# Norm factors of the attention input applied behind the products, in a two-layer trunk on one core

## The chip, the cores and the metric

One Trainium2 chip, one of its cores. The metric is the device time of one execution in microseconds (us). Before the change: median 762.31 us of 3 runs (762.25 to 763.36). The engines are TensorE (PE; PEld is its weight load), VectorE (DVE), ScalarE (ACT), GpSimd (POOL) and SyncE (SP). Each works through its own list of instructions in the order in which they were written down, and waits where an instruction's input is not ready.

## The reference

Two layers on 256 tokens of width 1024. Each layer normalises its input, multiplies it by one wide matrix, runs two attentions and gates, then a SwiGLU block:

```python
def rms_norm(x, g):
    y = x * rsqrt(mean(x * x, axis=-1) + EPS)     # token factor r, one per token
    return y * g                                  # column factor, one per column

h = rms_norm(x, attn_norm)
aq, ak, av, iq, ik, iw, bq, bk, bv, gates = split_cols(h @ w_in)
aq = apply_rope(rms_norm(aq, a_q_norm), cos, sin)         # 8 heads of 64; ak, bq, bk alike
iq = apply_rope(iq, cos, sin)                             # indexer: 4 heads of 64
ik = apply_rope(rms_norm(ik, idx_k_norm), cos, sin)
ya = sparse_attention(aq, ak, av, iq, ik, iw * 0.5, k_sel)  # 64 keys of each query by indexer score
yb = diff_attention(bq, bk, bv, lam)                      # then a norm per head
g_a, g_b = split(sigmoid(gates + gate_bias))
x = x + (g_a * (ya @ w_up_a) + g_b * (yb @ w_up_b)) @ w_out
h = rms_norm(x, ffn_norm)
gate, up = split(h @ w_ffn_in)
x = x + (silu(gate) * up) @ w_ffn_out
```

## The kernel before, in words

The 256 tokens stand in two tiles of 128, t = 0 and 1. A product is made from transposed activations (128 columns of the model and 128 tokens at a time) and weight units of 512 columns. For accuracy each fp32 product is three: both operands are split into a rounded high part and the rest, and `mm3` adds high·high (L240), high·low (L241) and low·high (L242). Activations are split after the transpose (`hilo`, or `hi` and `lo` in the first block), weights after their load: `split_half` makes the high part on ACT (L149) and the low part on DVE (L150). Raw weights lie in four buffers `raw`, split ones in four pairs `wh`, `wl`.

Names in the rows: a letter pair and a layer and a token tile, so `aq00` is the a-queries of layer 0, tile 0. `a0T` and `a1T` are the banks of the transposes of the attention input of layers 0 and 1, `a0h` and `a1h` the normalised input before it, `a0Th` and `a0Tl` the split halves. `gA`, `gB` are the gates, `ix` the indexer block (324 columns), `av`, `bv` the values, `fo` the last matrix of the SwiGLU.

Front of layer 0. The gain row is loaded to one partition and spread over 128 by a product with ones (`g0`, L374). For each token tile ACT sums the squares (L378), POOL makes r (L273, L276: a sum and a power), and DVE multiplies x by r and the gain (`norm_scale`, L309). PE transposes the result (L249), 4 chunks of 128 to a bank; ACT takes the high part of a whole bank (L713), DVE the low part (L716). The first block is half of gate A (`gA`), then `ix`. This stretch is in an order written out by hand for ACT and DVE (`first_block`); `part` makes the products of some chunks for one token tile.

Behind it comes a list of blocks for each layer (`BLOCKS`: ak, aq, av, bk, gA1, bq, bv, gB0, uA, gB1, uB). PE's order is the order of the program: `tok_block` makes a tile's product, hands the bank to an evacuation (`evac`), and `later` and `tick` put follow-up work on PE a set number of steps later (`QK_T` = 4 steps for the transposes of q and k). The instructions of the other engines are put in order by a scheduler outside the kernel from its own estimates, so a change of one place can change the order of DVE and ACT at others. Each of q and k ends in `qk_finish`: 8 sums of squares on ACT (one per head, L466), a power on POOL, for k a product by the factor on DVE (L471), for q a scaling of the factor (L474), then the rotation `rope` in three DVE steps (L455, L456, L458), and the transpose on PE. The indexer's finish (`idx_finish`) is alike; its scores are cut to the top 64 by eight rounds of `MAX` and `MATCH_REPLACE` on DVE (L529, L530), for two token tiles, `sc00m` on `nb` of tile 0, `sc01m` on that of tile 1.

At the end of layer 0 each half of x gets its `fo` product added (L920), ACT sums squares, POOL makes r, and `norm_scale` runs before the transposes of layer 1 (`a1T`).

Of the kernel before, what the change touches and what calls it, by code (L numbers as in the profile page):

```python
# [18 lines left out]
P = 128  # L19
# [17 lines left out]
GATE = IDX + IDXW + 1536  # L37

# [48 lines left out]
def tile_trunk(ctx, tc, x, angle, wpk, widx, gnorm, gbias, gqk, dlam, subln, const, out):  # L87
# [165 lines left out]
    cst = cp.tile([P, 3 * P], F32, name="cst")  # L253
    ident, cb = cst[:, :P], cst[:, P:3 * P]
# [3 lines left out]
    def load_x(t):  # L258
        nc.sync.dma_start(xs[t], x[0, t * P:(t + 1) * P, :])
# [38 lines left out]

    def norm_sum(N, t):
# [4 lines left out]
    def norm_scale(N, t, *parts):  # L304
        r = N["r", t]
        for c in parts or range(2):
            cs = slice(512 * c, 512 * c + 512)
            N["h"][t, c] = t2k([P, 512], f"{N['name']}h{t}{c}")
            nc.vector.scalar_tensor_tensor(N["h"][t, c], xs[t][:, cs], r, N["g"][c], ALU.mult, ALU.mult)  # L309

# [56 lines left out]
    g0b = [bank(f"g0{c}") for c in range(2)]  # L367

    def heat(n):
        nc.tensor.matmul(warm[:, :n], lhsT=idle[:, :P], rhs=idle[:, :n], start=True, stop=True)  # L370
# [12 lines left out]
    nc.gpsimd.dma_start(cb, const[:, P:])  # L383
# [11 lines left out]
    def angles():  # L395
        ve = nc.gpsimd
        ve.tensor_copy(posf, posi)
# [86 lines left out]
    def idx_finish(acc, l, t, I):  # L484
# [3 lines left out]
        nc.vector.tensor_scalar(iw, acc[:, 320:324], 0.5, None, ALU.mult)  # L488
        r = small(1, name + "r")
        nc.scalar.activation(junk[:, :64], acc[:, 256:320], AF.Square, scale=0.125, accum_out=r)  # L490
# [4 lines left out]
        nc.vector.tensor_scalar(kn, acc[:, 256:320], r, None, ALU.mult)  # L495
# [11 lines left out]
    def indexer(l, t, I):  # L507
# [10 lines left out]
        for j in range(2):  # L518
# [3 lines left out]
            nc.scalar.activation(rv, dv, AF.Relu, scale=0.125)  # L522
# [172 lines left out]
    def first_block(name, xT, evacs):  # L695
# [11 lines left out]
        def trans(t, g):  # L707
            b = bank(f"a0T{t}{g}")
            transposes(b, NA["h"][t, g], range(4))
            return [a[:, 4 * g:4 * g + 4, t * P:(t + 1) * P] for a in NA["T"]], heads(b, 4)  # L710

        def hi(d, b):
            nc.scalar.activation(d[0], b, AF.Copy)  # L713

        def lo(d, b):
            nc.vector.tensor_tensor(d[1], b, d[0].bitcast(F32), ALU.subtract)  # L716

        d0 = trans(0, 0)
        d1 = trans(1, 0)
        split_half(parts=2, between=lambda: (hi(*d0), lo(*d0)))  # L720
        hi(*d1)
        lo(*d1)
        split_half(parts=2)
        part(0, 0)
        part(0, 1, 0, 2)
        norm_scale(NA, 0, 1)
        split_half()
        d0 = trans(0, 1)
        hi(*d0)
        lo(*d0)  # L730
        part(0, 1, 2, 2)
        norm_scale(NA, 1, 1)
        split_half()
        part(1, 0, 0, 2)
        d1 = trans(1, 1)
        hi(*d1)
        lo(*d1)
        for _ in range(3):
            split_half()
        sines(turns)  # L740
        split_half()
# [13 lines left out]
    for l in range(DEPTH):  # L755
# [28 lines left out]
        def v_fin(i, t):  # L784
            return lambda acc: nc.scalar.activation(V8[i][:, t, :], acc, AF.Copy)
# [24 lines left out]
        def g_fin(g, c, t):  # L810
# [6 lines left out]
            def f(acc):  # L817
                nc.vector.tensor_tensor(G[0][:, t, cols[c]], acc, gb[g, c], ALU.add)
# [196 lines left out]
        for t in range(NT):  # L1015
            for c in range(2):
# [81 lines left out]
```

## Time and profile before

| | |
|---|---|
| median of 3 runs | 762.31 us (762.25 to 763.36) |
| profiled execution | 762.28 us |
| its span, first to last instruction | 760.5 us |
| PE busy | 751.3 us (99%) |
| PE weight load | 617.0 us (81%) |
| DVE busy | 573.6 us (75%) |
| ACT busy | 470.6 us (62%) |
| POOL busy | 108.7 us (14%) |
| HBM read | 152.89 MB, 202 GB/s over the span |

Busy shares are over the span. A matmul's time in the trace is longer than the distance to the next, since matmuls overlap in a pipeline; the distance between starts is what a product costs PE. An entry in square brackets behind a row is the time that the engine stood idle before it and what released it.

### The profile page before, as it was taken

How to read it: one execution, taken by the hardware profiler on the slowest of the kernel's cores; microseconds unless marked ns; L12 is line 12 of the kernel's file. 1: busy time of each engine (PE TensorE's matmuls, PEld its weight loads, DVE VectorE, ACT ScalarE, POOL GpSimd, SP SyncE). 2: the span in 40 equal slices, each digit the busy share in tenths (PEclk: the TensorE clock that was granted, in tenths of full speed). 3: DMA queues.
4: the chain of work that ended last, by engine and by line, in shares of the span. 5: the costliest groups of instructions: out<-in, count | busy, mean ns of one | idle time of the engine just before them, and what ended most of it. 6: DMA issues, size and time to landing. Idle time of an engine off the chain costs nothing.

```text
span 760.5 us, 10268 instructions
## 1 busy us (share of the span) xinstructions
PE 751.3 (99%) x3638; PEld 617.0 (81%) x3638; DVE 573.6 (75%) x885; ACT 470.6 (62%) x938; POOL 108.7 (14%) x135
## 2 busy tenths in 40 slices
PE   8999999999999999999999999999999999999998
PEld 5877888888888888888888787888888888888886
DVE  5999757768777777777768987667777877787673
ACT  5766597655665656656547676876546666565660
POOL 5741220010031100010001411200002010000100
PEclk9999999999999999999999999999999999999999
DMA  9744635436568888977746273443476599868921
GB/s 317 290 168 166 235 125 183 162 115 234 206 167 264 234 275 258 275 231 221 240 150 221 91 242 125 177 170 125 166 272 213 152 218 293 255 236 270 231 102 55
DMA packets 45061, 154.60 MB, mean 203 GB/s; under 512 B 5409, under 2 KB 6177, under 8 KB 45010
## 3 DMA queue, kind: packets, MB, share of 16 engines
q1 hardware_dynamic: 40320, 136.97, 49.1%
q0 software_dynamic: 4688, 16.98, 12.7%
q8 instruction: 28, 0.46, 0.2%
q14 instruction: 23, 0.19, 0.1%
q10 hardware_dynamic: 2, 0.00, 0.0%
HBM read 152.89 MB, written 1.05 MB: 202 GB/s over the span
## 4 chain that ended last, share of the span: by engine, by line
PE 90%; DVE 5%; ACT 1%; DMA 1%; POOL 1%; issue 1%; SPq 0%; ACTq 0%; DVEq 0%
PE fo L242 5%; PE fo L240 5%; PE fo L241 5%; PE fi L242 5%; PE fi L241 5%; PE fi L240 5%; PE qX L242 3%; PE qX L240 3%; PE qX L241 3%; PE gB L240 2%; PE gB L242 2%; PE wo L242 2%; PE gB L241 2%; PE wo L240 2%; PE wo L241 2%; PE gA L240 2%
## 5 line engine op out<-in xcount | busy, mean ns | idle before, releaser
L240 PE MATMUL fo<-wh,aTh 128*128 128x512 f32 (+1 forms) x100 | 38.2, 382 | 0.0
L241 PE MATMUL fo<-wl,aTh 128*128 128x512 f32 (+1 forms) x100 | 38.1, 381 | 0.0
L242 PE MATMUL fo<-wh,aTl 128*128 128x512 f32 (+1 forms) x100 | 38.1, 381 | 0.0
L197 ACT ACTIVATE wh<-raw1q 128x1024 fp32r<-128x1024 f32 (+1 forms) x24 | 30.0, 1268 | 8.3 <-DMA raw1q<-wpk 7.0
L197 ACT ACTIVATE wh<-raw0q 128x1024 fp32r<-128x1024 f32 (+1 forms) x24 | 30.0, 1268 | 8.1 <-DMA raw0q<-wpk 5.6
L201 DVE TENSOR_TENSOR wl<-raw0q,wh 128x2048 fp32r<-128x2048 f32 x15 | 34.2, 2284 | 0.6 <-ACT wh L197 0.6
L201 DVE TENSOR_TENSOR wl<-raw1q,wh 128x2048 fp32r<-128x2048 f32 x15 | 34.2, 2284 | 0.6 <-ACT wh L197 0.6
L240 PE MATMUL fo<-wh,aT 128*128 128x512 f32 x80 | 32.0, 400 | 0.0
L240 PE MATMUL fi<-wh,f0Th 128*128 128x512 f32 x80 | 31.9, 399 | 0.0
L240 PE MATMUL fi<-wh,f1Th 128*128 128x512 f32 x80 | 31.9, 399 | 0.0
L242 PE MATMUL fo<-wh,aT 128*128 128x512 f32 x80 | 31.3, 391 | 0.0
L242 PE MATMUL fi<-wh,f1Tl 128*128 128x512 f32 x80 | 31.2, 391 | 0.0
L242 PE MATMUL fi<-wh,f0Tl 128*128 128x512 f32 x80 | 31.2, 390 | 0.0
L241 PE MATMUL fo<-wl,aT 128*128 128x512 f32 x80 | 31.2, 390 | 0.0
L241 PE MATMUL fi<-wl,f0Th 128*128 128x512 f32 x80 | 31.2, 390 | 0.0
L241 PE MATMUL fi<-wl,f1Th 128*128 128x512 f32 x80 | 31.2, 390 | 0.0
L201 DVE TENSOR_TENSOR wl<-raw1fo,wh 128x2048 fp32r<-128x2048 f32 x11 | 25.1, 2285 | 3.4 <-ACT wh L197 3.4
L201 DVE TENSOR_TENSOR wl<-raw0fo,wh 128x2048 fp32r<-128x2048 f32 x11 | 25.1, 2285 | 3.4 <-ACT wh L197 3.4
L197 ACT ACTIVATE wh<-raw0fo 128x1024 fp32r<-128x1024 f32 x22 | 22.0, 1050 | 7.9 <-issue 4.0
L197 ACT ACTIVATE wh<-raw1fo 128x1024 fp32r<-128x1024 f32 x22 | 22.0, 1049 | 7.6 <-issue 4.1
L240 PE MATMUL wo<-wh,mTh 128*128 128x512 f32 x64 | 25.6, 400 | 0.0
L242 PE MATMUL wo<-wh,mTl 128*128 128x512 f32 x64 | 25.0, 391 | 0.0
(1050 smaller groups left out, 2490.2 us busy)
## 6 DMA issues: line engine op xcount, KB each, us to landing
raw0q<-wpk SPq DMA_DIRECT2D x24, 512.0 KB, 6.0
raw1q<-wpk SPq DMA_DIRECT2D x24, 512.0 KB, 5.6
raw0fo<-wpk SPq DMA_DIRECT2D x22, 512.0 KB, 6.2
raw1fo<-wpk SPq DMA_DIRECT2D x22, 512.0 KB, 6.0
raw0fi<-wpk SPq DMA_DIRECT2D x20, 512.0 KB, 4.2
raw1fi<-wpk SPq DMA_DIRECT2D x20, 512.0 KB, 4.4
raw0q<-wpk POOLq DMA_DIRECT2D x12, 512.0 KB, 6.8
raw1q<-wpk POOLq DMA_DIRECT2D x12, 512.0 KB, 7.6
```

The lines of the kernel that those rows point to most:

```text
L197: nc.scalar.activation(hi[:, k * w:k * w + w], raw[:, k * w:k * w + w], AF.Copy)
L201: nc.vector.tensor_tensor(ready[n][1], stage.pop(("raw", n)), ready[n][0].bitcast(F32), ALU.subtract)
L240: nc.tensor.matmul(acc, lhsT=sh, rhs=mh, start=first, stop=False, skip_group_check=more)
L241: nc.tensor.matmul(acc, lhsT=sh, rhs=ml, start=False, stop=False, skip_group_check=more)
L242: nc.tensor.matmul(acc, lhsT=sl, rhs=mh, start=False, stop=last, skip_group_check=more)
```

## The change

The norm's two factors are put elsewhere. x itself is transposed. In layer 0 the column factor (the gain) is a column per chunk (`gcol`) and is multiplied in when the transposed chunk is split into high and low; in layer 1 it is multiplied by x as soon as each half of x has its `fo` product (`gain_only`). The token factor r is applied behind the products, at each evacuation: q and k take their squares of r·0.125·acc (a pointer as ACT's scale) and multiply r into their own factor, the indexer multiplies by r where it reads the bank, v's copy has r as its scale, and the gate sums become acc·r + bias. The squares of layer 0 stand behind the first splits. Loads: identity, gain columns, positions and frequencies come in one DMA on ACT's queue; x comes in four halves with gate A's first weights between; the constants `cb` go to SP's queue. The gain product is gone, two more products on ones stand in its place, and the first activation table loaded is Sin's in place of Square's.

```diff
-    g0 = b8([P, D], "grow")[0:1]
-    load_x(0)
-    nc.scalar.dma_start(g0, gnorm[0:1, :])
-    nc.scalar.activation(junk[:, :8], mhalf, AF.Square)
-    nc.gpsimd.dma_start(ident, const[:, :P])
-    load_x(1)
-    for n in range(2):
-        raw_of(seq[n])
...
+    nc.scalar.dma_start(cst[:, :CONST], const[:, :CONST])
+    load_x(0, 0)
+    raw_of(seq[0])
+    load_x(1, 0)
+    load_x(0, 1)
+    load_x(1, 1)
+    raw_of(seq[1])
+    nc.sync.dma_start(cb, const[:, CONST:])
     for n in range(2, 4):
         raw_of(seq[n])
+    nc.scalar.activation(junk[:, :8], mhalf, AF.Sin)
...
-    heat(256)
-    for c in range(2):
-        nc.tensor.matmul(g0b[c], lhsT=idle[0:1, :P], rhs=g0[:, 512 * c:512 * c + 512], start=True, stop=True)
-    NA = new_norm("a0", g0b)
-    for t in range(NT):
-        NA["ss"][t] = small(2, f"a0ss{t}")
-        nc.scalar.activation(junk, xs[t], AF.Square, scale=1.0 / 32, accum_out=NA["ss"][t][:, :1])
-        NA["r", t] = small(1, f"a0r{t}")
-        rsqrt(NA["r", t], NA["ss"][t][:, :1])
-        norm_scale(NA, t, 0)
+    for _ in range(3):
+        nc.tensor.matmul(warm[:, :256], lhsT=idle[:, :P], rhs=idle[:, :256], start=True, stop=True)
+    NA = new_norm("a0", None)
...
+    def row_factors(N, t):
+        rows[t] = N["r", t], small(1, f"{N['name']}e{t}", "e", 4)
+        nc.gpsimd.tensor_scalar(rows[t][1], N["r", t], 0.125, None, ALU.mult)
...
+    def gain_only(N, t, c):
+        cs = slice(512 * c, 512 * c + 512)
+        N["h"][t, c] = t2k([P, 512], f"{N['name']}h{t}{c}")
+        nc.vector.tensor_tensor(N["h"][t, c], xs[t][:, cs], N["g"][c], ALU.mult)
...
+        rt, r8 = rows[t]
         for h in range(8):
-            nc.scalar.activation(junk[:, 64 * h:64 * h + 64], acc[:, 64 * h:64 * h + 64], AF.Square, scale=0.125,
+            nc.scalar.activation(junk[:, 64 * h:64 * h + 64], acc[:, 64 * h:64 * h + 64], AF.Square, scale=r8,
                                  accum_out=r[:, h:h + 1])
         rsqrt(r, r)
         if rq is None:
+            nc.vector.tensor_scalar(r, r, rt, None, ALU.mult)
...
-            nc.vector.tensor_scalar(r, r, 0.125, None, ALU.mult)
+            nc.vector.tensor_scalar(r, r, rt, 0.125, ALU.mult, ALU.mult)
...
+            b = [bank(f"a0T{t}{g}{i}") for i in range(2)]
+            for c in range(4):
+                transposes(b[c % 2][:, c // 2 * P:], xs[t], [4 * g + c])
+            return t, g, b
+
+        def chunk(d, c):
+            t, g, b = d
+            hi, lo = [a[:, 4 * g + c, t * P:(t + 1) * P] for a in NA["T"]]
+            b, gain = b[c % 2][:, c // 2 * P:c // 2 * P + P], gcol[:, 4 * g + c:4 * g + c + 1]
+            nc.scalar.activation(hi, b, AF.Copy, scale=gain)
+            nc.vector.scalar_tensor_tensor(lo, b, gain, hi.bitcast(F32), ALU.mult, ALU.subtract)
+
+        def halves_with(d):
+            chunk(d, 0)
+            split_half(parts=2, between=lambda: chunk(d, 1))
+            chunk(d, 2)
+            split_half(parts=2, between=lambda: chunk(d, 3))
...
+        halves_with(trans(0, 0))
+        part(0, 0, 0, 1)
+        d = trans(1, 0)
+        chunks(d)
+        part(0, 0, 1, 3)
+        halves_with(trans(0, 1))
+        part(0, 1)
+        d = trans(1, 1)
+        chunks(d)
         part(1, 0, 0, 2)
+        squares(0)
+        for _ in range(2):
             split_half()
+        squares(1)
         sines(turns)
-        split_half()
+        for _ in range(2):
+            split_half()
...
-            return lambda acc: nc.scalar.activation(V8[i][:, t, :], acc, AF.Copy)
+            return lambda acc: nc.scalar.activation(V8[i][:, t, :], acc, AF.Copy, scale=rows[t][0])
...
-                nc.vector.tensor_tensor(G[0][:, t, cols[c]], acc, gb[g, c], ALU.add)
+                nc.vector.scalar_tensor_tensor(G[0][:, t, cols[c]], acc, rows[t][0], gb[g, c], ALU.mult, ALU.add)
...
                 if not last:
+                    gain_only(NA, t, c)
                     norm_half(NA, t, c)
                 tick()
             if not last:
                 norm_sum(NA, t)
-                norm_scale(NA, t)
+                row_factors(NA, t)
```

The scheduler's order changes with it. On DVE, around the rope of `aq00` in layer 0 (`aq00q` is the rotated tile, L458 its last sum; the numbers behind the names tell buffers apart), stood before:

```order
L455 TENSOR_TENSOR aq00q<-aq_577,cg_265 128x512
L529 MAX sc00m_500<-nb_158 128x8
L456 TENSOR_TENSOR aq00b<-aq_577,sg_266 128x512
L530 MATCH_REPLACE nb_158<-sc00m_500,nb_158 128x128
L458 TENSOR_TENSOR aq00q<-aq00q,aq00b 128x512
L529 MAX sc00m_503<-nb_158 128x8
L529 MAX sc01m_552<-nb_159 128x8
L530 MATCH_REPLACE nb_158<-sc00m_503,nb_158 128x128
L530 MATCH_REPLACE nb_159<-sc01m_552,nb_159 128x256
L531 TENSOR_SCALAR nb_158<-nb_158 128x128
L529 MAX sc01m_555<-nb_159 128x8
L533 TENSOR_TENSOR nb_158<-nb_158,cst 128x128
```

On DVE at the same place stands now (L532 is before's L529, L533 its L530, L534 its L531, L536 its L533):

```order
L456 TENSOR_TENSOR aq00b<-aq_603,sg_290 128x512
L532 MAX sc00m_528<-nb_140 128x8
L532 MAX sc01m_578<-nb_141 128x8
L533 MATCH_REPLACE nb_140<-sc00m_528,nb_140 128x128
L533 MATCH_REPLACE nb_141<-sc01m_578,nb_141 128x256
L534 TENSOR_SCALAR nb_140<-nb_140 128x128
L532 MAX sc01m_581<-nb_141 128x8
L536 TENSOR_TENSOR nb_140<-nb_140,cst 128x128
L533 MATCH_REPLACE nb_141<-sc01m_581,nb_141 128x256
L458 TENSOR_TENSOR aq00q<-aq00q,aq00b 128x512
```

The last sum of the rope has moved behind eight rows of the top-k selection, which stood behind it before.

The second place is DVE's work between the first weights and the indexer's (`wl` of `raw0ix` are the two pairs of weight splits of the ix block, `gA_...<-gA_...` the evacuation of the two token tiles of gate A). Before:

```order
L150 TENSOR_TENSOR wl_250<-raw0ix_97,wh_249 128x648 x2
L150 TENSOR_TENSOR wl_256<-raw0ix_100,wh_255 128x648 x2
L438 TENSOR_TENSOR dl_132<-dl_132 128x128
L818 TENSOR_TENSOR gA_166<-gA_169,gA00b 128x512
L440 TENSOR_REDUCE e_276<-dl_132 128x2
L818 TENSOR_TENSOR gA_166<-gA_170,gA00b 128x512
```

On DVE at the same place now:

```order
L152 TENSOR_TENSOR wl_267<-raw0ix_95,wh_266 128x648 x2
L833 SCALAR_TENSOR_TENSOR gA_148<-gA_151,a0r_261,gA00b 128x512
L833 SCALAR_TENSOR_TENSOR gA_148<-gA_152,a0r_274,gA00b 128x512
L152 TENSOR_TENSOR wl_283<-raw0ix_98,wh_282 128x648 x2
L438 TENSOR_TENSOR dl_114<-dl_114 128x128
```

The second pair of ix splits has moved behind both gate sums.

## Rows read from the trace of the kernel before

**Rows 1.** The page: busy time of the engines (us, share of the span, instructions), and the share of each engine in the chain of work that ended last.

```profile
PE 751.3 (99%) x3638; PEld 617.0 (81%) x3638; DVE 573.6 (75%) x885; ACT 470.6 (62%) x938; POOL 108.7 (14%) x135
...
PE 90%; DVE 5%; ACT 1%; DMA 1%; POOL 1%; issue 1%; SPq 0%; ACTq 0%; DVEq 0%
```

**Rows 2.** What PE waited for over the whole execution: PE's waiting instruction, what it waited for, us in total, times, longest us.

```profile
PE ix01T L249 <- DVE ix01q L497: 0.9, 1, 0.9
PE a0T L249 <- DVE a0h L309: 0.9, 2, 0.7
PE aq10T L249 <- DVE aq10q L458: 0.8, 1, 0.8
PE a1T L249 <- DVE a1h L309: 0.7, 1, 0.7
PE ak L241 <- DVE wl L150: 0.4, 1, 0.4
PE bk10T L249 <- DVE bk10q L458: 0.2, 1, 0.2
```

**Rows 3.** PE in order of time, the front up to the first ix product; columns: start us, us of one or of the group, engine, line, operation, out<-in, shape and count.

```profile
1.44 1.22 PE L370 MATMUL warm<-idle 128*128 128x256 f32 x2 [1.44 <-DVE idle L365]
2.59 3.78 PE L374 MATMUL g<-grow,idle 1*128 1x512 f32 x4
7.10 1.11 PE L249 MATMUL a0T<-cst,a0h 128*128 128x128 f32 x4 [0.73 <-DVE a0h L309]
...
9.15 0.78 PE L240 MATMUL gA<-wh,a0Th 128*128 128x512 f32 x1
...
10.58 0.63 PE L240 MATMUL gA<-wh,a0Th 128*128 128x512 f32 x1
11.01 0.51 PE L241 MATMUL gA<-wl,a0Th 128*128 128x512 f32 x1
11.36 0.40 PE L242 MATMUL gA<-wh,a0Tl 128*128 128x512 f32 x1
11.59 0.40 PE L240 MATMUL gA<-wh,a0Th 128*128 128x512 f32 x1
...
22.11 0.31 PE L240 MATMUL ix<-wh,a0Th 128*128 128x324 f32 x1
```

**Rows 4.** ACT in order of time (squares of x, first weight split), and DVE (weight splits of gA and ix, a gate sum), same columns; in brackets the idle time before and its releaser.

```profile
4.13 1.06 ACT L378 ACTIVATE junk<-x 128x1024 f32<-128x1024 f32 x1 [1.36 <-DMA x<-x]
...
5.44 1.06 ACT L378 ACTIVATE junk<-x 128x1024 f32<-128x1024 f32 x1 [0.16 <-DMA x<-x]
...
7.38 0.63 ACT L149 ACTIVATE wh<-raw0gA 128x512 fp32r<-128x512 f32 x1 [0.79 <-DMA raw0gA<-wpk]
...
8.25 0.68 DVE L150 TENSOR_TENSOR wl<-raw0gA,wh 128x512 fp32r<-128x512 f32 x1
...
23.76 0.83 DVE L150 TENSOR_TENSOR wl<-raw0ix,wh 128x648 fp32r<-128x648 f32 x1 [1.64 <-ACT wh L149]
...
26.21 0.68 DVE L818 TENSOR_TENSOR gA<-gA,gA00b 128x512 f32<-128x512 f32 x1
```

**Rows 5.** POOL, DVE and PE in order of time around the transpose of aq00, layer 0 (ak01r is the factor of ak's tile 1).

```profile
46.49 1.68 POOL L276 TENSOR_TENSOR ak01r<-ak01r,mhalf 128x8 f32<-128x8 f32 x1
...
48.20 0.69 DVE L471 TENSOR_TENSOR ak01xn<-ak,ak01r 128x512 f32<-128x512 f32 x1
...
56.73 0.16 DVE L474 TENSOR_SCALAR rqaq<-rqaq 128x8 f32<-128x8 f32 x1
...
58.46 0.69 DVE L458 TENSOR_TENSOR aq00q<-aq00q,aq00b 128x512 f32<-128x512 f32 x1
59.06 0.29 DVE L529 MAX8 sc00m<-nb 128x8 f32<-128x128 f32 x1
...
61.30 1.21 DVE L150 TENSOR_TENSOR wl<-raw0bk,wh 128x1024 fp32r<-128x1024 f32 x1
...
59.35 0.60 PE L249 MATMUL aq00T<-cst,aq00q 128*128 128x128 f32 x4
```

**Rows 6.** ACT: two copies of 512 columns grouped by line and shape (durations in ns: least, median, most), with one pointer as scale and without; then in order of time an exponential with two pointers, and a square without one, each with its accumulator read.

```profile
L673 ACT ACTIVATE yB<-Bf00T,sb x1: 688/688/688, 163.8 to 163.8; 128x512 fp32r<-128x512 f32 x1
...
L785 ACT ACTIVATE KV<-av x4: 577/588/598, 62.8 to 447.9; 128x512 f32<-128x512 f32 x4
...
71.52 0.49 ACT L553 ACTIVATE A000m<-A000m,A000x,rqaq 128x128 f32<-128x128 f32 x1 [2.26 <-DVE A000x L551]
71.92 0.19 ACT L553 ACTIVATION_READ_ACCUMULATOR A000m<-A000m,A000x,rqaq 128x1 f32 x1
...
160.98 0.27 ACT L658 ACTIVATE junk<-Bpv 128x128 f32<-128x128 f32 x1
161.14 0.20 ACT L658 ACTIVATION_READ_ACCUMULATOR junk<-Bpv 128x1 f32 x1
```

**Rows 7.** POOL and DVE in order of time at the layer boundary, tile 0 (a1r is the token factor of layer 1).

```profile
379.58 0.57 POOL L276 TENSOR_TENSOR a1r<-a1r,mhalf 128x1 f32<-128x1 f32 x1
...
380.18 1.41 DVE L309 SCALAR_TENSOR_TENSOR a1h<-x,a1r,ga 128x512 f32<-128x512 f32 x2 [1.91 <-POOL a1r L276]
```

**Rows 8.** DVE and PE in order of time at the transpose of aq11, layer 1.

```profile
438.19 0.68 DVE L458 TENSOR_TENSOR aq11q<-aq11q,aq11b 128x512 f32<-128x512 f32 x1
...
439.01 0.63 PE L249 MATMUL aq11T<-cst,aq11q 128*128 128x128 f32 x4
```

More of the change, by code (lines that the diff above doesn't have):

```diff
@@ L37 @@
 GATE = IDX + IDXW + 1536
+CONST = P + 8 + NT + 32
 LAM_INIT = [0.8 - 0.6 * math.exp(-0.3 * l) for l in range(DEPTH)]
@@ L86, in tile_trunk @@
 @with_exitstack
-def tile_trunk(ctx, tc, x, angle, wpk, widx, gnorm, gbias, gqk, dlam, subln, const, out):
+def tile_trunk(ctx, tc, x, wpk, widx, gnorm, gbias, gqk, dlam, subln, const, out):
     nc = tc.nc
@@ L252, in tile_trunk, with load_x @@
     xs = [cp.tile([P, D], F32, name=f"x{t}") for t in range(NT)]
-    cst = cp.tile([P, 3 * P], F32, name="cst")
-    ident, cb = cst[:, :P], cst[:, P:3 * P]
+    cst = cp.tile([P, CONST + 2 * P], F32, name="cst")
+    ident, gcol, posi, ivf = [cst[:, a:b] for a, b in ((0, P), (P, P + 8), (P + 8, P + 8 + NT), (P + 8 + NT, CONST))]
+    cb = cst[:, CONST:]
     mhalf = cp.tile([P, 8], F32, name="mhalf")
     nc.gpsimd.memset(mhalf, -0.5)
-    def load_x(t):
-        nc.sync.dma_start(xs[t], x[0, t * P:(t + 1) * P, :])
+    def load_x(t, c):
+        cs = slice(512 * c, 512 * c + 512)
+        nc.sync.dma_start(xs[t][:, cs], x[0, t * P:(t + 1) * P, cs])
     def row(src, r, c, name):
@@ L297, in norm_half @@
         nc.scalar.activation(junk[:, :512], xs[t][:, cs], AF.Square, scale=1.0 / 32, accum_out=N["ss"][t][:, c:c + 1])
+    rows = {}
+    def row_factors(N, t):
+        rows[t] = N["r", t], small(1, f"{N['name']}e{t}", "e", 4)
+        nc.gpsimd.tensor_scalar(rows[t][1], N["r", t], 0.125, None, ALU.mult)
     def norm_sum(N, t):
@@ L302, in norm_sum, with norm_scale @@
         rsqrt(r, ss[:, 0:1], ss[:, 1:2])
-    def norm_scale(N, t, *parts):
+    def norm_scale(N, t):
         r = N["r", t]
-        for c in parts or range(2):
+        for c in range(2):
             cs = slice(512 * c, 512 * c + 512)
@@ L366, in tile_trunk @@
     warm = bank("warm")
-    g0b = [bank(f"g0{c}") for c in range(2)]
-    def heat(n):
-        nc.tensor.matmul(warm[:, :n], lhsT=idle[:, :P], rhs=idle[:, :n], start=True, stop=True)
-    heat(256)
-    for c in range(2):
-        nc.tensor.matmul(g0b[c], lhsT=idle[0:1, :P], rhs=g0[:, 512 * c:512 * c + 512], start=True, stop=True)
-    NA = new_norm("a0", g0b)
-    for t in range(NT):
-        NA["ss"][t] = small(2, f"a0ss{t}")
-        nc.scalar.activation(junk, xs[t], AF.Square, scale=1.0 / 32, accum_out=NA["ss"][t][:, :1])
-        NA["r", t] = small(1, f"a0r{t}")
-        rsqrt(NA["r", t], NA["ss"][t][:, :1])
-        norm_scale(NA, t, 0)
-    nc.gpsimd.dma_start(cb, const[:, P:])
+    for _ in range(3):
+        nc.tensor.matmul(warm[:, :256], lhsT=idle[:, :P], rhs=idle[:, :256], start=True, stop=True)
+    NA = new_norm("a0", None)
     C0 = consts_in(0)
@@ L396, in angles @@
         ve = nc.gpsimd
-        ve.tensor_copy(posf, posi)
+        ve.tensor_copy(posf, posi.bitcast(I32))
         rr = t2k([P, 512], "angle")
@@ L487, in idx_finish @@
         iw = I["iw"][t]
-        nc.vector.tensor_scalar(iw, acc[:, 320:324], 0.5, None, ALU.mult)
+        rt, r8 = rows[t]
+        nc.vector.tensor_scalar(iw, acc[:, 320:324], rt, rt, ALU.mult, ALU.mult)
         r = small(1, name + "r")
-        nc.scalar.activation(junk[:, :64], acc[:, 256:320], AF.Square, scale=0.125, accum_out=r)
+        nc.scalar.activation(junk[:, :64], acc[:, 256:320], AF.Square, scale=r8, accum_out=r)
         rsqrt(r, r)
@@ L494, in idx_finish @@
         kn = q[:, 384:448]
-        nc.vector.tensor_scalar(kn, acc[:, 256:320], r, None, ALU.mult)
+        nc.vector.tensor_scalar(kn, acc[:, 256:320], r, rt, ALU.mult, ALU.mult)
         rope(heads(q[:, 256:320], 1), heads(kn, 1), cg[:, 2, :], sg[:, 2, :], 1, name + "k")
@@ L521, in indexer @@
             rv = heads(rd, 2)[:, :, :K]
-            nc.scalar.activation(rv, dv, AF.Relu, scale=0.125)
+            nc.scalar.activation(rv, dv, AF.Relu, scale=0.0625)
             for pr in range(2):
@@ L707, in trans @@
         def trans(t, g):
[L708 to L726, printed above, removed]
-        split_half()
[L728 to L733, printed above, removed]
+            b = [bank(f"a0T{t}{g}{i}") for i in range(2)]
[8 more added lines that the diff above has]
+            nc.vector.scalar_tensor_tensor(lo, b, gain, hi.bitcast(F32), ALU.mult, ALU.subtract)
@@ new lines, in halves_with, with squares @@
+        def halves_with(d):
[3 more added lines that the diff above has]
+            split_half(parts=2, between=lambda: chunk(d, 3))
+        def squares(t):
+            NA["ss"][t] = small(2, f"a0ss{t}")
+            nc.scalar.activation(junk, xs[t], AF.Square, scale=1.0 / 32, accum_out=NA["ss"][t][:, :1])
+            NA["r", t] = small(1, f"a0r{t}")
+            rsqrt(NA["r", t], NA["ss"][t][:, :1])
+            row_factors(NA, t)
@@ L734, in first_block, with chunks @@
+        def chunks(d):
+            for c in range(4):
+                chunk(d, c)
+        halves_with(trans(0, 0))
[7 more added lines that the diff above has]
+        chunks(d)
         part(1, 0, 0, 2)
[L735 to L738, printed above, removed]
+        squares(0)
+        for _ in range(2):
             split_half()
+        squares(1)
@@ L740, in first_block @@
         sines(turns)
-        split_half()
+        for _ in range(2):
+            split_half()
         lays[0] = layer_consts(0, *C0)
@@ L1029, in tile_trunk @@
                 norm_sum(NA, t)
-                norm_scale(NA, t)
+                row_factors(NA, t)
 def pack(w_in, w_up_a, w_up_b, w_out, w_ffn_in, w_ffn_out):
@@ L1074 @@
     tri = i[None, :] > i[:, None]
-    const = np.zeros((P, 3 * P), np.float32)
+    invf = (np.float32(1) / (10000.0 ** (np.arange(0, 64, 2) / 64)).astype(np.float32)).astype(np.float32)[None]
+    const = np.zeros((P, CONST + 2 * P), np.float32)
     const[:, :P] = np.eye(P)
-    const[:, 2 * P:3 * P][tri] = NEG
-    invf = (np.float32(1) / (10000.0 ** (np.arange(0, 64, 2) / 64)).astype(np.float32)).astype(np.float32)[None]
+    const[:, P:P + 8] = f(attn_norm)[0].reshape(8, P).T
+    const[:, P + 8:P + 8 + NT] = f(positions).astype(np.int32).reshape(NT, P).T.copy().view(np.float32)
+    const[:, P + 8 + NT:CONST] = invf
+    const[:, CONST + P:][tri] = NEG
     arrays = {
         "x": f(x), "wpk": wpk, "widx": widx,
-        "angle": np.concatenate([f(positions).reshape(NT, P).T, np.tile(invf.view(np.int32), (P, 1))], axis=1),
         "gnorm": np.concatenate([f(attn_norm), f(ffn_norm)], axis=0),
```

4 lines of the change are left out of this document (1 added, 3 removed).

## The prediction

> **What bounds the kernel now.** I read four views in this order. First the page's busy shares and the chain that ended last: the reader is to see that TensorE (PE) is busy for 751.3 of 760.5 us and carries 90% of the chain [rows 1]. So a change is worth only what it does to PE's own work and to PE's waits; time saved on another engine counts where PE waits for that engine and nowhere else. Second the list of what PE waits for [rows 2]: six waits besides that for the very first operand, 3.9 us together, all for VectorE (DVE). Third PE's first 12 us [rows 3], because there the matmuls run at two paces. Fourth the order in time of DVE, ScalarE (ACT) and GpSimd (POOL) just ahead of those of PE's transposes that now come without a wait, to see how late their inputs already are [rows 5, 8]. The profiled execution took 762.28 us, 760.5 of span and 1.78 around it; the median is 762.31, so I add to 762.28 and count the two as one number.
>
> **Front, up to the first ix product.** In before PE does a 256-column product on ones, a product of one row (the broadcast of the gain), and 8 transposes, and its first real product starts at 9.15. [...] (The page's row of the granted clock shows full speed throughout; the pitch of the products says otherwise, and I go by the pitch.) The ix products start at 22.11. After the change no square, no rsqrt and no gain product stands ahead of the transposes. A whole x tile of 512 KB landed at 4.13 and the next at 5.44, 1.31 later, and the first weights at 7.38 [rows 4]; half a tile is there by 4.13 at the latest, the weights, now behind half a tile and not two, 1.5 x 1.31 earlier, at 5.4; by the same rate x's other parts land at 7.3 to 8.6 and gA's second weights by 11, ahead of their use. Three heats of about 1.2 us from 1.44 end near 5.0; the first transpose ends at 5.3, its chunk's split on ACT (0.4, an estimate from the 0.69 of a Copy four times as wide [rows 6]) and the first weight half (0.63 [rows 4]) follow: first product at about 6.3, 2.85 earlier. Against that, DVE must make the low half of the weights (0.68 [rows 4]) and of the chunk before the second and third product, about 1.0 us of waiting, and 3 groups of transposes instead of 2 stand between the products (0.36 more). With the whole stretch at full pace the ix products start at 6.3 + 48 x 0.2275 + 3 x 0.36 + 1.3 = 19.6, 2.5 earlier than before. If the clock rises at 11.2, as before, about 8 products and one group of transposes run slow: 8 x 0.2 + 0.3 = 1.9 lost, start at 21.5, 0.6 earlier. [...] I take a rise within the first products, at a loss of 0.6 out of 1.9: **-1.9** (-2.5 to -0.6).
>
> [...]
>
> **The ix gate.** On DVE the second pair of ix weight splits now stands behind both gate sums, and the second of these needs PE's last gA product. A sum is 0.68 (+0.06 for the added factor), a split 0.83 [rows 4]; PE has four chunks x 3 products of 324 columns, 0.2275 x 324 / 512 = 0.144 each [rows 3], 1.7 us, before it needs the split. If only the second sum is left when that product ends, 0.74 + 0.83 hides behind 1.7; if both are (the first also waits for r, which is now computed after the second tile's split, and stands behind two ix splits), 0.74 more shows: **+0.7** (0 to +0.8). Of before's waits the 0.9 at ix01T goes (DVE has one weight split fewer ahead of its copy) and I leave the 0.4 at ak [rows 2]: **-0.9** (-1.3 to 0). Until the av products PE is thus 2.1 us ahead of before.
>
> **The rope of aq, layer 0, token tile 0.** In before DVE works without a break from 48.20 to past 61.30; it starts there when POOL has finished ak01's factor (48.17) [rows 5]. aq00q is summed at 58.46 to 59.15, and PE starts its transpose at 59.35 without a wait, 0.2 after [rows 5]. In after the sum stands behind eight more top-k rows, those that ran from 59.06 to 61.30 in before: 2.24 us later. Nothing hides this: these rows wait for nothing but DVE itself, and PE has no other work until the transpose, since its order is fixed. The chain in front also gets longer: ak01's squares now take their scale through a pointer. One Copy of 512 columns with one pointer takes 688 ns, without 577 to 598: 0.09; two exponentials' pointers cost (71.92 - 71.52) - (161.14 - 160.98) = 0.24 against a square of the same 128 columns: 0.12 each [rows 6]. Eight squares: 0.72 (0 if ACT hides it between the pairs, 0.96 by the exponentials). And the added product by r on 128x8, 0.16 by itself, 0.07 beside others [rows 5]. Together 2.24 + 0.72 + 0.1 - 0.2 of slack = **+2.9** (2.1 to 3.2). The front does not soften this: ak01's squares start when PE has finished ak01, so a PE that is ahead pulls the chain along.
>
> [...]
>
> **Layer boundary.** The gain is now multiplied in as soon as each x + fo is there, and the token factor later; a1T no longer waits for POOL's power (ends at 380.15) and the two scalings after it [rows 7]. The wait of 0.7 [rows 2] goes, and nothing new stands in its place, because the power is needed only by the first evacuation a block later: **-0.7** (-0.8 to -0.4).
>
> **The other ropes.** The same +0.8 of ACT and DVE stands in all 16 finishes. Most have over 2 us of cover. aq10T (0.8) and bk10T (0.2) wait already [rows 2], so nothing covers theirs; aq11T's input ends 0.14 ahead of it [rows 8]. But the DVE queue there begins earlier as a1h comes earlier, and a wait at one takes part of the next. I take half of 3 x 0.8, less what aq01 and aq11 get back: **+1.0** (0 to 2.2). The gate sums, 16 x 0.06, and the two-pointer scale of v lie beside PE's work: +0.2 (0 to 0.4) for the one product that waits for a v just evacuated.
>
> The hi/lo split itself costs nothing on PE: 16 short splits on ACT and DVE instead of 4 long ones run beside gA's products, and if that cover were gone it would be the +0.36 and the 1.0 counted above. The table load that falls away stood ahead of no wait of PE's [rows 2], so nothing is counted for it.
>
> Sum: -1.9 + 0.7 - 0.9 + 2.9 - 0.7 + 1.0 + 0.2 = +1.3: **763.6 us**. A measurement of this kernel tells about 0.2%, 1.5 us, from no change; so this is "within", near its upper edge. With the ends of the front alone it is 763.0 to 764.9; its own range, with the smaller terms, 762.7 to 764.4.
>
> **Rivals.**
> (1) *The clock rises as late as before* (11.2), because the heats end before 5 and the first product then stands with rests among transposes. For it: busy time alone did not raise it in before; the first token half has only three products before it stops for four transposes again. [...] The front is then -0.6: 764.9, slower than before. It decides from a rise later than about 8.5.
> (2) *The pointers are hidden* between square and accumulator read. The front, 2.2 at aq00T and nothing at the other ropes: -1.9 + 0.7 - 0.9 + 2.2 - 0.7 + 0.2 = -0.4, 761.9. Against it: the exponentials' rows stand back to back and show no hiding [rows 6].
> (3) *DVE leads*: DVE comes to aq00's rope so early that the eight rows are done before PE needs the sum. Place: DVE between ak01xn and aq00q; it decides from a lead of 2.9 us over before. Price: the +2.9 goes, and with such a lead half of the +1.0: 760.2, faster. For it: before's DVE does two weight splits (1.2 each) between these rows, and the new order has moved one wl split behind the ix copies. Against it: ak01xn is tied to PE's last ak product, and 13 us of dense DVE work follow in before.
>
> **How the numbers follow.** Forecast 50%, (1) 27%, (2) 13%, (3) 10%. Of the forecast's 50 about 33 fall below 763.8 (within), 17 above; (1) gives 24 slower and 3 within; (2) 12 within and 1 faster; (3) 8 faster and 2 within. Faster 0.09, within 0.50, slower 0.41. The range leaves out about half of (3) and the end of (1) where all pointers cost 0.12: 761.0 to 765.6.
>
> **What will show it.** The start of gA's first product (6.3) and of ix's (20.2), and where the pitch falls from 0.43 to 0.23. A wait of PE at aq00T of about 2.9 for L458, with eight top-k rows right before that sum; under 2.3 says the pointers are hidden, none says rival 3. No wait at a1T and none at ix01T. The squares of ak and aq 0.09 further apart per head than now. The forecast is wrong if aq00T's wait is missing, if the ix products start after 22, or if a new wait over 1 us stands behind 62 us.

## The result and the profile after

The changed kernel takes 770.43 us (median of 4 runs, 769.51 to 770.97), the kernel before 762.35 in the same comparison: 1.010 times as long, 95% interval 1.0087 to 1.0113. It is slower by 8 us where 1.3 were forecast, outside the range. The profiled execution took 769.51 us, with a span of 767.7.

The page's busy times and chain, as in [rows 1]:

```profile
PE 752.1 (98%) x3638; PEld 617.5 (80%) x3638; DVE 575.9 (75%) x903; ACT 484.1 (63%) x951; POOL 111.1 (14%) x137
...
PE 82%; DVE 7%; ACT 5%; POOL 2%; issue 2%; DMA 1%; SPq 0%; ACTq 0%; DVEq 0%; POOLq 0%
```

PE is busy for nearly as long as before (752.1 for 751.3 us); its share of the chain has fallen from 90 to 82%. So most of the loss, 6.4 of the 7.2 us by which the span is longer, is time in which PE waits. What PE waits for, in the order and with the columns of [rows 2]:

```profile
PE aq00T L251 <- DVE aq00q L458: 4.0, 1, 4.0
...
PE ak L243 <- DVE wl L152: 1.2, 1, 1.2
PE aq10T L251 <- DVE aq10q L458: 1.1, 1, 1.1
...
PE Apv L601 <- ACT A003eT L593: 0.6, 1, 0.6
...
PE ak11T L251 <- DVE nb L534: 0.5, 1, 0.5
PE bk10T L251 <- DVE bk10q L458: 0.4, 1, 0.4
PE Apv L601 <- ACT A002eT L593: 0.4, 1, 0.4
```

The waits at ix01T and a1T are gone, as forecast; one of 4.0 us has come at aq00T, and two for ACT (A002eT, A003eT) that the prediction did not name. (Waits of 0.3 us and less, and those of the front, are left out here.) PE in order of time, the front and the stretch around aq00's transpose, as in [rows 3, 5]:

```profile
1.44 2.93 PE L382 MATMUL warm<-idle 128*128 128x256 f32 x6 [1.44 <-DVE idle L379]
4.82 1.10 PE L251 MATMUL a0T<-cst,x 128*128 128x128 f32 x4 [0.45 <-DMA cst<-const]
6.70 0.50 PE L242 MATMUL gA<-wh,a0Th 128*128 128x512 f32 x1 [0.78 <-ACT wh L151]
...
8.67 0.39 PE L243 MATMUL gA<-wl,a0Th 128*128 128x512 f32 x1
8.90 0.39 PE L244 MATMUL gA<-wh,a0Tl 128*128 128x512 f32 x1
...
61.79 1.09 PE L251 MATMUL aq00T<-cst,aq00q 128*128 128x128 f32 x4 [3.97 <-DVE aq00q L458]
...
63.95 0.63 PE L242 MATMUL av<-wh,a0Th 128*128 128x512 f32 x1
64.38 0.63 PE L243 MATMUL av<-wl,a0Th 128*128 128x512 f32 x1
...
67.31 0.40 PE L244 MATMUL av<-wh,a0Tl 128*128 128x512 f32 x1
67.54 0.40 PE L242 MATMUL av<-wh,a0Th 128*128 128x512 f32 x1
```

The first product starts at 6.70 and the pitch is 0.23 at once (8.67 to 8.90): in this execution the clock is up before the first product, and ix starts at 19.69. But behind the 4.0 us of rest the products are 0.43 apart (63.95 to 64.38) until 67. The same in the view by stretches, whose columns are the stretch, its length, PE's busy time and products, the granted clock, the DMA share and GB/s:

```profile
60.00:64.00 4.00, 2.21 (x8) 0.55 0.17 70
64.00:66.00 2.00, 2.00 (x6) 0.50 0.00 0
66.00:68.00 2.00, 2.00 (x7) 0.70 0.00 0
68.00:70.00 2.00, 2.00 (x10) 1.00 0.47 129
```

The clock granted is 0.50 of full speed behind the rest (64 to 66), and back at 1.00 from 68. Each product behind the rest takes some 0.2 longer (0.43 for 0.23), and the way from aq00T to aq01T is 2.3 us longer (8.5 for 6.2).

Where the whole time went is best seen by the start of the same work on PE in the two traces (us):

| PE starts | before | after | after - before | step |
|---|---|---|---|---|
| ix, layer 0 | 22.11 | 19.69 | -2.42 | -2.4 |
| ak | 29.22 | 27.38 | -1.84 | +0.6 |
| first scores (sc00d) | 40.01 | 37.91 | -2.10 | -0.3 |
| aq00T | 59.35 | 61.79 | +2.44 | +4.5 |
| aq01T | 65.57 | 70.30 | +4.73 | +2.3 |
| second Apv | 108.06 | 114.18 | +6.12 | +1.4 |
| aTT (second group, first block of the SwiGLU) | 222.63 | 229.19 | +6.55 | +0.4 |
| fo behind a1T | 382.06 | 387.61 | +5.55 | -1.0 |
| ak11T | 426.18 | 432.37 | +6.19 | +0.6 |
| bk10T | 457.90 | 465.09 | +7.19 | +1.0 |
| end | | | +7.2 | 0.0 |

Three stretches make the loss: aq00T with the slow products behind it (6.8), the attention at 104 to 118 (1.4), and layer 1's finishes (1.6). DVE in order of time: the start of its unbroken work, and the end of the rope of aq00, which answers to [rows 5]:

```profile
41.51 0.23 DVE L471 TENSOR_SCALAR ak00r<-ak00r,a0r 128x8 f32<-128x8 f32 x1 [1.90 <-POOL ak00r L280]
...
58.72 0.29 DVE L532 MAX8 sc00m<-nb 128x8 f32<-128x128 f32 x1
...
60.63 0.41 DVE L533 MATCH_REPLACE8 nb<-sc01m,nb 128x256 f32<-128x256 f32 x1
60.95 0.69 DVE L458 TENSOR_TENSOR aq00q<-aq00q,aq00b 128x512 f32<-128x512 f32 x1
```

DVE has POOL's factor of ak00 at 41.51; the last sum of aq00q runs at 60.95, behind the eight top-k rows from 58.72 to 60.95. ACT in order of time, the first two squares of ak00 with their new scale:

```profile
34.75 0.30 ACT L467 ACTIVATE junk<-ak,a0e 128x64 f32<-128x64 f32 x1
...
35.04 0.31 ACT L467 ACTIVATE junk<-ak,a0e 128x64 f32<-128x64 f32 x1
```

They start 0.29 apart; in the trace of before it was 0.195. The same places in the trace of before, the first square of ak00 on ACT and the start of DVE's unbroken work:

```profile
35.60 0.23 ACT L466 ACTIVATE junk<-ak 128x64 f32<-128x64 f32 x1 [0.96 <-PE ak L242]
...
41.15 0.69 DVE L471 TENSOR_TENSOR ak00xn<-ak,ak00r 128x512 f32<-128x512 f32 x1 [0.33 <-POOL ak00r L276]
```

And the layer boundary, DVE and PE in order of time, for [rows 7]:

```profile
385.25 0.69 DVE L325 TENSOR_TENSOR a1h<-x,ga 128x512 f32<-128x512 f32 x1
...
386.82 1.03 PE L251 MATMUL a1T<-cst,a1h 128*128 128x128 f32 x8
387.61 0.48 PE L242 MATMUL fo<-wh,aTh 128*128 128x512 f32 x1
```

The last product by the gain that they need ends at 385.94, 0.9 ahead of the transposes a1T, which start without a wait; the products behind them come 0.79 later, where it was 1.07 with the wait before (380.99 to 382.06).

### The profile page after: what moved, and what is told of

It reads as the page before. It is cut to its first block, busy times and chain, and to the rows that moved or that the text cites. A ratio compares the mean times of both kernels' runs of the same rounds, so it can differ in the third digit from the quotient of the medians.

```text
span 767.7 us, 10307 instructions
## 1 busy us (share of the span) xinstructions
PE 752.1 (98%) x3638; PEld 617.5 (80%) x3638; DVE 575.9 (75%) x903; ACT 484.1 (63%) x951; POOL 111.1 (14%) x137
## 4 chain that ended last, share of the span: by engine, by line
PE 82%; DVE 7%; ACT 5%; POOL 2%; issue 2%; DMA 1%; SPq 0%; ACTq 0%; DVEq 0%; POOLq 0%
PE fo L244 5%; PE fo L243 5%; PE fo L242 5%; PE fi L242 4%; PE fi L244 4%; PE fi L243 4%; PE qX L244 3%; PE qX L243 3%; PE qX L242 3%; PE gB L242 2%; PE gB L244 2%; PE gB L243 2%; DVE wl L152 2%; ACT junk L467 2%; PE wo L242 2%
```

## The experiments

My theory after the result (A): the loss at aq00T is the moved sum (about 2.2) and a longer chain of squares and factors before it; the rest that it makes lets the clock fall, which costs 2.3 more. Rivals: (B) the pointers and added operations in all 16 finishes (the norm and rope of each q and k) make the loss, and the order only shows it; (C) the slow products have a cause of their own. All times are medians, with the ratio to the kernel before on the same chip; in brackets the 95% interval.

**rope_first: the moved sum undone.** The top-k rows (the last round of sc00 and all of sc01, `behind`) are issued behind the sum again (and the first weight splits of bk are tied behind it too, where they stand in both kernels):

```diff
-        rope(heads(q, 8), heads(src, 8), cg[:, i, :], sg[:, i, :], 8, name)
+        done = rope(heads(q, 8), heads(src, 8), cg[:, i, :], sg[:, i, :], 8, name)
+        if name == "aq00":
+            with tc.issue_after(done.ins):
+                for fn in behind:
+                    fn()
```

> The changed kernel with one thing put back: on VectorE the last sum of aq00's rope (layer 0, tile 0) is issued ahead of the eight top-k rows again; nothing else of the change is touched, nothing is left out. Theory A (the moved sum and the clock): TensorE's wait at aq00T falls from 4.0 to about 1.8 us, after so short a rest the products stay at 0.23 us apart, and both losses go: 770.4 - 2.2 - 2.3 = 765.9. Theory B (the pointers and added operations spread over all finishes make the loss, the order only shows it): the wait falls by less than 1, the other waits stay, 769 to 770. Theory C (the slow products have another cause than the rest): 770.4 - 2.2 = 768.2, with products 0.43 apart behind aq00T still.

Measured: 766.02, 1.0043 [1.0027, 1.0059]. PE at aq00T, and a product behind it:

```profile
59.64 0.63 PE L253 MATMUL aq00T<-cst,aq00q 128*128 128x128 f32 x4 [1.85 <-ACT wh L152]
...
60.80 0.39 PE L244 MATMUL av<-wh,a0Th 128*128 128x512 f32 x1
61.03 0.39 PE L245 MATMUL av<-wl,a0Th 128*128 128x512 f32 x1
```

The wait is 1.85 in place of 3.97 (the row names a Copy of ACT, but DVE's sum of aq00q, from 58.80 to 59.49, is what the transpose needs), the products behind it keep 0.23, and 4.4 us of the median are gone (5.1 when each kernel is set against before in its own comparison), for A's 4.5. B and C are out for this part.

**imm_scale: the pointers and the factor r taken out of the norms of q and k.**

```diff
-            nc.scalar.activation(junk[:, 64 * h:64 * h + 64], acc[:, 64 * h:64 * h + 64], AF.Square, scale=r8,
+            nc.scalar.activation(junk[:, 64 * h:64 * h + 64], acc[:, 64 * h:64 * h + 64], AF.Square, scale=0.125,
...
-            nc.vector.tensor_scalar(r, r, rt, None, ALU.mult)
...
-            nc.vector.tensor_scalar(r, r, rt, 0.125, ALU.mult, ALU.mult)
+            nc.vector.tensor_scalar(r, r, 0.125, None, ALU.mult)
```

> The changed kernel with the squares of q and k taken with the immediate scale 0.125 again and without the factor r in q's and k's norms: a norm divides r out, so only the place of the small EPS under the root changes. The rest of the change stays. The scheduler then puts the rope's last sum ahead of the top-k rows by itself. Theory A: squares 0.195 us apart per head in place of 0.29; wait at aq00T 1.0 to 1.8 and no slow products; the waits at Apv, ak11T, aq10T, aq11T as in before; the boundary's gain of 1.1 stays: 761.0 (760.0 to 762.5). Theory B: the same waits shrink but the 2.3 of slow products and half of the wait at aq00T stay: 765 to 766.

Measured: 761.55, 0.9984 [0.9974, 0.9994], faster than before. PE's waits:

```profile
PE aq10T L251 <- DVE aq10q L458: 1.3, 1, 1.3
PE ak L243 <- DVE wl L152: 1.3, 1, 1.3
PE aq01T L251 <- ACT wh L151: 1.2, 1, 1.2
...
PE aq00T L251 <- DVE aq00q L458: 0.5, 1, 0.5
```

aq00T waits 0.5, and those at Apv and ak11T are gone. In this order it is aq01's sum that stands behind eight top-k rows, hence its 1.2 (the row again names ACT; the sum runs from 64.32 to 65.00, the transpose starts at 65.15). Against rope_first this version saves 4.5 more, so B is right for that part: the pointers and products in the finishes, together with the order of DVE and ACT that comes with them, cost as much as the moved sum and its fall of the clock.

**fill_rest: PE kept busy in its rest.**

```diff
             b = bank(name + "T")
+            for _ in range(8 if name == "aq00" else 0):
+                nc.tensor.matmul(b[:, :256], lhsT=ident, rhs=cst[:, :256], start=True, stop=True)
             transposes(b, q, range(4))
```

> The changed kernel with eight products of 256 columns (identity times constants, overwritten afterwards) put on TensorE just ahead of aq00's transposes, where it rests for 4.0 us; the result is the same. Theory A (the rest lets the clock fall): the transposes start when they did, but the products behind them come at 0.23 us apart: 770.4 - 2.3 = 768.1. Theory C (the slow products have another cause, for instance contention with what runs beside them): slow products stay, 770.4.

Measured: 768.58, 1.0067 [1.0051, 1.0083]. PE:

```profile
59.25 3.61 PE L483 MATMUL aq00T<-cst 128*128 128x256 f32 x16
63.25 0.66 PE L251 MATMUL aq00T<-cst,aq00q 128*128 128x128 f32 x4 [0.39 <-DVE aq00q L458]
...
64.21 0.40 PE L244 MATMUL av<-wh,a0Tl 128*128 128x512 f32 x1
64.44 0.40 PE L242 MATMUL av<-wh,a0Th 128*128 128x512 f32 x1
```

The transposes come no earlier for it (their input sets them; they come 1.5 later than after's, since this execution lost 1.6 in the front), and the products behind them are 0.23 apart: the way from aq00T to aq01T takes 6.0 us for after's 8.5. By the medians 1.9 us of the 8 are gone (2.5 when each kernel is set against before in its own comparison) by nothing but idle work: with the rest filled the products keep 0.23 apart beside the same neighbours, so it was the rest that let the clock fall here. C is out. Not all that the clock gives back stays: bk00T, which did not wait in after, now waits 1.1, while the waits at Apv are nearly gone (0.1 is left).

**one_heat: one product on ones at the start, not three.** `range(3)` becomes `range(1)`.

> The changed kernel with one product on ones at the start in place of three; the rest the same. It asks what the front is worth. Theory A (VectorE sets the time of aq00T, so a start of TensorE that is earlier or later up to there only changes its rest): products of gA run slow until about 11, ix starts about 1.8 us later than now (21.5 in place of 19.7), the rest at aq00T shrinks by as much, to about 2.2, and the end is no later: 770.4 if the clock falls there all the same, 768.1 if it doesn't. Theory D (the front counts in full): 772.2. If the clock rises as early without the two products, all is as now, 770.4, and ix starts at 19.7.

Measured: 771.61, 1.0108 [1.0093, 1.0123]. In its trace ix starts at 20.97, 1.3 later than after, aq00T at 63.03, 1.2 later, and PE rests 3.94 there all the same. So my claim that a later front only shortens the rest falls: ak00's squares start at 36.00 for 34.75, DVE's chain comes as much later, and the front counts (D). This rests on the trace; the intervals of the two medians overlap. Whether two heats more raise the clock earlier can't be read from it. Over the twelve kernels with three heats that were profiled (the change itself and eleven of the experiments), the pitch is 0.23 from the first product in six; in four it falls to that only between 9.8 and 12.6, in one_heat at 10.1. In the other two (fill_rest, rope_act) the clock was up and fell again: PE rested 1.1 us ahead of its first product, and the clock granted was 1.00 from 6 to 8 us, 0.50 from 8 to 11 and 1.00 again from 12 (in rope_act the products are 0.43 apart from 9.37 to 11.07, 0.23 from 11.46).

**mul_only and rope_act: what in the finishes costs 4.5.** mul_only is imm_scale with the added products by r kept. rope_act is rope_first with one weight split moved on ACT:

```diff
-            nc.scalar.activation(hi[:, c], raw[:, c], AF.Copy)
+            with tc.issue_after(copied_A["A003"].ins) if seq[i] == (0, "gB0", 0) else ExitStack():
+                nc.scalar.activation(hi[:, c], raw[:, c], AF.Copy)
```

> As imm_scale, with the added products by r on VectorE kept (one of 128x8 for each k, r in place of 0.125's second factor for q); only the pointers of the squares are gone, so q and k come out multiplied by r once too often. ScalarE's order of instructions is that of imm_scale. Theory P (the pointers, and the order that the scheduler derives from the longer squares, cost what lies between rope_first and imm_scale, 4.5 us): 762.0 (761.3 to 762.8), no wait at Apv. Theory M (the added products by r cost at least half of it): 763.8 or more.

Measured: 763.83, 1.0017 [1.0007, 1.0027]: M's number. But its trace gives M only a part. aq00's sum stands ahead of the top-k rows again, by the pointers' absence alone: they touch none of these instructions, and yet they are what moved the sum. It has no wait at Apv or ak11T, so those 2.0 us belong to the squares' pointers; and of what it has more than imm_scale, 1.6 us are another fall of the clock, behind a wait of 1.82 at aq01T, where imm_scale waits 1.18:

```profile
66.61 0.63 PE L251 MATMUL aq01T<-cst,aq01q 128*128 128x128 f32 x4 [1.82 <-DVE aq01q L458]
...
68.29 0.63 PE L243 MATMUL av<-wl,a0Th 128*128 128x512 f32 x1
68.72 0.63 PE L244 MATMUL av<-wh,a0Tl 128*128 128x512 f32 x1
...
71.56 0.40 PE L242 MATMUL av<-wh,a0Th 128*128 128x512 f32 x1
71.79 0.40 PE L243 MATMUL av<-wl,a0Th 128*128 128x512 f32 x1
```

The wait is longer where the products by r are kept, but DVE's order differs too, so the products' own share is not shown; the clock does the rest. A split of the 4.5 into pointers and products in whole numbers stays open.

> As rope_first, and on ScalarE the first weight split of gB0 is issued behind the copies A010eT and A003eT again, where it stood before the change; the squares keep their pointers. Nothing is left out. Theory O (the loss of 0.9 at the second Apv, layer 0, is the moved weight split of about 1.0 us): that wait of 0.6 goes, 766.0 - 0.8 = 765.2, and the wait of 0.3 to 0.4 at the first Apv, where the order is as before, stays. Theory P (it is the eight squares, 0.76 longer, alone): both waits stay, 766.0.

Measured: 766.44, 1.0048 [1.0032, 1.0064], as rope_first. The wait at the second Apv is gone as O said, and it is back at the next copy:

```profile
PE Apv L622 <- ACT A011eT L614: 0.8, 1, 0.8
```

ACT itself is the bound in this stretch (in after busy for 15.97 of the 16 us from 100 to 116), with 16 squares 0.1 longer each: the order only chooses which copy is late. Neither theory had that.

**bound_undone: the layer boundary as in before, in imm_scale.** In layer 1 `norm_scale` again, and ones as row factors.

> As imm_scale with the layer boundary as in before: in layer 1 the token factor and the gain are multiplied into x together, after GpSimd's power, and a factor of one is applied behind the products. It asks what the gain at the boundary is worth. Theory G (given back): the wait of 0.7 at a1T returns and the gain of 1.1 there is gone, but the wait at aq10T falls from 1.3 to 0.7 and the ones behind it too, so the end is 0.3 to 0.6 later than imm_scale. Rival (it counts in full): 1.1 later.

Measured: 764.34, 1.0013 [1.0004, 1.0022], 2 us behind imm_scale, some of it a late rise of the clock in the front (1.4 in its trace). At the transposes a1T its trace loses 0.9 against imm_scale, and 0.3 more from there to the products behind them, and the wait at aq10T is 1.3 in both: the gain is not given back there. G falls, and the boundary's 1.2 counts in full.

**Versions: best_a, best_b, imm_c, best_c, best_d.** best_a adds to imm_scale an indexer without r, the second ak split ahead of ix00's wait, and tile 1's top-k rounds behind aq's ropes; best_b the first weight split ahead of the first chunk's; imm_c and best_c are imm_scale and best_b (imm_c with the split too) with a product on ones behind the first transposes; best_d moves a bk split behind aq10's last sum.

> A version made from what the first four runs showed; it computes the reference. From the change: the front without the gain product and the gain at the boundary. From before: immediate scales, and no r in the norms of q, k and the indexer (a norm divides it out, and a positive factor per query leaves the selection alone). New: the second ak weight split is put ahead of ix00's wait for GpSimd, and tile 1's top-k rounds are issued behind the ropes of aq. Against imm_scale the wait of 1.3 at ak and of 1.2 at aq01T should go, and most of the 1.3 at aq10T: 761.5 - 1.2 - 1.0 - 0.8 = 758.5 (757.5 to 760). If VectorE is the bound in this stretch, the waits only move to the next transposes or to the first attention scores: 761.

> As best_a, and at the very front the first weight split on ScalarE stands ahead of the first chunk's split, since the weights may have landed before the transposes are done. If they have: first product at 6.1 in place of 6.7, 0.6 less than best_a in the end. If they land later than 5.7: no change or 0.3 more.

> As imm_scale, with two things at the very front: the first weight split on ScalarE ahead of the first chunk's split, and a product on ones (192 columns) between the first transposes and the first product, where TensorE rested 0.8 to 1.3. Theory H (work without a rest from 1.44 on makes the clock rise before or within the first products in every execution, where the profiles so far show the rise anywhere from the first product to 12.6): median 0.5 to 1.0 below imm_scale's 0.9984 of before, so 0.997 to 0.9975, 760.7, and executions less spread. If the rise depends on something else: 0.998 as imm_scale.

> As best_b with the same product on ones between the first transposes and the first product. Theory H: 0.9975 of before or below, 760.5. If the waits that best_a and best_b moved from ak and aq01 to bk00 are no gain (VectorE is the bound from 41 to 61 whatever the order), the same as imm_c.

> As best_c with one instruction moved: in layer 1 the first weight split of bk (1.13 us on VectorE) is issued behind the last sum of aq10's rope and no longer ahead of it. The wait of 1.27 at aq10T should fall to 0.15. If nothing behind it waits for what now comes later, the end is 1.1 earlier than best_c's: 0.9973 - 0.0014 = 0.996 of before, 760.2 where before takes 763.2. Rival: aq11T or bk10T, whose inputs come behind the moved split, wait in its place and give it back, 0.9973.

Measured: best_a 762.60, 0.9990 [0.9980, 1.0000]; best_b 761.79, 0.9986 [0.9977, 0.9996]; imm_c 762.19, 0.9984 [0.9975, 0.9992]; best_c 761.41, 0.9973 [0.9963, 0.9984]; best_d 761.32, 0.9983 [0.9974, 0.9992]. H falls: with the same work in the front, best_c's products are at full pace from the first, though PE rested 1.07 before them, and imm_c's only from 10 (0.23 apart from 10.15), with a rest of 0.28. The weight split in front gains nothing, as the weights land later than I took (ACT gets them at 5.88 in best_b). best_a's waits at ak and aq01 did go, and 1.1 of it came back at bk00T. best_d shows the same on two rows, PE's waits in best_c and then in best_d:

```profile
PE aq10T L251 <- DVE aq10q L459: 1.3, 1, 1.3
PE bk00T L251 <- DVE bk00q L459: 1.1, 1, 1.1
```

```profile
PE bk00T L253 <- DVE bk00q L461: 1.1, 1, 1.1
...
PE bk10T L253 <- DVE bk10q L461: 0.8, 1, 0.8
...
PE aq10T L253 <- DVE aq10q L461: 0.3, 1, 0.3
```

The 1.0 that left aq10T is 0.8 at bk10T, and bk10T then starts at the same time as before the move: the rival. DVE is the bound in this stretch (its rows in best_c show no idle time from 420.20 to past 433.85), and its order only moved the wait. The best versions are 0.2 to 0.3% faster than before; best_c, best_d and imm_scale can't be told apart.

## Why the prediction was wrong, step by step

- *Front, -1.9:* measured -2.4, within its bounds (first product at 6.70 for 6.3, ix at 19.69 for 20.2), with the clock up before the first product. The -1.9 holds a rise of the clock within the first products at a loss of 0.6, which was my estimate: no run shows what decides when the clock rises. The runs show the pitch at 0.23 from the first product in six of the twelve profiles with three heats; in four the rise is late, as rival 1 had it, and in two the clock fell again in the front.
- *Ix gate, +0.7:* +0.6, right. *ix01T and ak, -0.9:* -0.3. The wait at ix01T went; that at ak grew from 0.4 to 1.2, because the split that it needs stands on DVE behind ix00's rope, which waits for POOL. I had left that wait as it was.
- *aq00T, +2.9:* 4.5 with the 0.4 at ak00T. The step's 2.24 for the eight rows is right (2.1 by rope_first). What failed is "a PE that is ahead pulls the chain along", by which PE's lead was to come through whole. I tied DVE's dense work to ak01's squares and its start at 48.20; in both traces it starts with ak00's factor, at 41.51 in after, 0.4 later than before (41.15). PE's lead was 2.4 at ix, but the waits for the ix and ak splits came off it, and ak00's squares start only 0.85 earlier (34.75 for 35.60). On the way from there the change adds more than that: 0.7 for the longer squares, 0.5 at POOL (37.30 to 41.48 for 37.44 to 41.11) and 0.3 for the product by r. So DVE's chain started late, and the lead of PE became rest.
- *The fall of the clock, +2.3:* in no term. I weighed the clock for the front alone and never asked what a new wait does to it. The trace shows what it does: a clock of 0.50 behind the 4.0 us of rest, and products 0.43 apart for 0.23. This term and the one above (4.5 for 2.9) make 3.9 of the 5.9 us between forecast and profile.
- *Gates and v, +0.2:* +1.8 (1.4 by Apv, 0.4 by the aTT transposes). The step looked at the gate sums and v's copy, and not at what ACT has to do beside 16 longer squares. The cost of a pointer, 0.09, was right (0.29 for 0.195 between squares); "most have over 2 us of cover" was said of the finishes, and the copies of ACT that stand behind their squares have no such cover.
- *Boundary, -0.7:* -1.2 at the boundary itself, 0.9 at a1T and 0.3 behind it (-1.0 in the table, whose stretch also holds 0.2 of small losses), and it counts in full. The step had priced the wait and not the products behind it. *Other ropes, +1.0:* +1.6, within its bounds; ak11T is one that I had not named.
- *Rivals:* the pointers were not hidden (2; 0.29 for 0.195 between squares), DVE did not lead (3). The range ended at 765.6 because no case let two losses meet: a wait, and the clock that falls for it. The median lies 0.9 above the profiled execution; a late rise or a fall of the clock in the front would make that much (1.2 to 2.4 in traces of the experiments), but no profile of this kernel shows it.

## What to carry to other kernels

A new wait on TensorE can cost twice: here 4.0 us for its length, and 2.3 for the products behind it, 0.43 us apart in place of 0.23 while the clock granted was 0.50. Before a scheduler's new order is priced, ask which earlier event starts the dense work of the waiting engine: a lead of TensorE comes through only as far as it reaches that event, less what the change adds on the way to it (here 0.85 of 2.4 reached it, and 1.5 was added). A longer instruction on one engine can move the scheduler's order on another, as the pointers on ACT did to DVE here. And a factor that a later norm divides out need not be applied at all: that took away the whole loss here (imm_scale), with the gains at the front and at the boundary kept.

## What was not expected of the hardware

The clock fell behind rests of 3.97 and 3.94 us, and once behind one of 1.82 (mul_only), but not behind 1.85 (rope_first); in the front it fell behind rests of 1.1 (fill_rest, rope_act), but not behind 1.34 (best_b): the length of the rest alone does not decide. The page's row of the granted clock shows full speed in the first 11 us of before, where the products are 0.43 apart, as behind the rest in after, and not 0.23. And the same POOL operation on 128x8 took from 0.23 to 2.42 us, longest while DVE split weights of 1024 columns. Two rows of POOL in after, in order of time:

```profile
37.30 2.42 POOL L277 TENSOR_SCALAR ak00r<-ak00r 128x8 f32<-128x8 f32 x1 [3.45 <-ACT junk L467]
...
57.76 0.24 POOL L277 TENSOR_SCALAR rqaq<-rqaq 128x8 f32<-128x8 f32 x1 [3.44 <-ACT junk L467]
```

Both are the same operation, for the factor of ak00 and of aq01; the first ran from 37.30 to 39.72, while two of DVE's splits of aq's weights ran (37.25 to 39.61). Of the sixteen such operations in after, seven took 0.23 to 0.26 us; each of the nine longer ones ended 0.1 us after an operation of DVE that ran beside it, as 39.72 after 39.61 here. That DVE's operations hold it that long is my estimate from these nine, not shown: no run changes this alone.
